# Hybrid decoder trunk: two more groups per layer by seven products, and the input's quarter sums formed in other places

## The chip, the cores and the metric

The kernel runs on one core of one Trainium2 chip. The metric is the device time of one execution in microseconds (us), the median of several runs. The parts of the core are named as in the profile: PE is TensorE's matmuls, PEld its weight loads, DVE is VectorE, ACT is ScalarE, POOL is GpSimd, and SP is SyncE, which here only issues transfers (DMAs).

## The reference

Two layers run one after the other on 512 tokens of width 2048. A layer normalises its input, multiplies it by one wide matrix `w_in` of 7696 columns, and feeds the columns to three groups of heads: a short gated convolution, a stick-breaking attention with eight heads of 128, and a gated linear attention (GLA) with four heads. Each has a gate path through SiLU. The three outputs stand side by side, go through `w_out` and are added to the layer's input.

```python
    h = _rmsnorm(x, norm_g).astype(x.dtype)
    proj = h @ w_in
    ...
    y_conv = _short_conv(cv_h, cv_b, cv_c, conv_w, conv_b) * jax.nn.silu(cv_g.astype(f32))
    ...
    y_sb = _stick_breaking(q, k, v) * jax.nn.silu(sb_g.astype(f32))
    ...
    y_gla = _rmsnorm(o, gla_on_g).reshape(b, s, GLA_W) * jax.nn.silu(gl_g.astype(f32))

    mix = jnp.concatenate([y_conv, y_sb, y_gla], axis=-1).astype(x.dtype)
    return x + mix @ w_out
```

## The kernel before, in words

**Groups of weights.** The columns of `w_in` and `w_out` are taken 256 at a time. One such block of 2048 rows by 256 columns is a group; there are 38 in a layer, 76 in all, and they are multiplied in one fixed order. In a layer it is: GLA's V0 and V1 (V1 carries the 16 low-rank columns too), GLA's Q and K, GLA's two gates G0 and G1, the first half of the convolution (its groups H, C, G, B), four times the attention's V, Q, K and gate, the second half of the convolution, and the eight groups of `w_out`.

**Precision.** Every operand is split into a high and a low float16 part, and a product is three matmuls: high by high, high by low, low by high. The splitting is work of ACT (the high part, a scaled copy) and DVE (the low part, scaled value minus high part).

**Two ways to multiply a group.** The plain way for groups whose result stands with columns on the partitions (`project_cols`, L625 to L627) takes 2 column blocks x 16 row blocks x 3 = 96 matmuls of 128x512. The other way, `seven` (L677 by columns, L680 by tokens), cuts the input into four quarters (tokens 0 to 255 and 256 to 511, rows 0 to 1023 and 1024 to 2047) and the weights into four (the two row halves, the two column blocks), and forms the four quarters of the result from seven products of sums of quarters in place of eight. By columns that is 7 x 8 x 3 = 168 matmuls of 128x256. Which groups go this way is in the table `SEVEN`; before, there are 39.

**What `seven` needs of the weights.** A plain group's two staged halves of 1 MB (tag `st`, four buffers) are split into four tiles `w` (`whi` L419, `wlo` L423, 128x1024 each). For `seven`, `right` (L428 to L452) makes seven such tiles (ACT L436, DVE L437), with four additions in place on the staged halves between them (L440, L441, L444, L445). The pool of `w` tiles has six buffers for all groups. A group is prepared about one group ahead: its squares are summed for a scale (ACT L344, an all-reduce on POOL, L357), and its tiles are made as buffers come free. The fetch of a staged half (L332, on SP) waits until the half that it overwrites has been split.

**What `seven` needs of the input.** Four sums of the input's quarters, in float16 parts and transposed. `x_sums` (L768) makes them once per layer, and it is issued behind V1's last weight split: eight additions on the normalised input `xt` in place (`column_sums`, L763 to L766, 128x1024 each), eight splits (ACT L780, DVE L781), each into a borrowed tile, and sixteen transposes by DMA on SP (L789), which write the sums into two tiles `s` that take over the buffers of `xt`. In `quarters`, sum 1 is the left operand of product 1, sum 0 of product 3, sums 2 and 3 of products 4 and 5; products 0, 2 and 6 take quarters of the input itself. The products are computed in the order 0, 1, 3, 2, 4, 5, 6.

**The results of `seven`.** Three PSUM banks `psp` serve all groups. By columns, two copies on ACT (L691, L727) and five additions on DVE (L720, L723, L731, and L735 twice), each 128x256, bring the quarters into an SBUF tile; a plain group is read from PSUM by what follows, for a gate by the chain of L820 to L827.

**Borrowed tiles.** The split sums go to tiles whose tags belong to other steps and have one or two buffers, handed on in the order of the program: `g` (the gates), `zw` and `raw` (`attd` of GLA, which POOL clears at L975; `raw` is also `Pc`, GLA's running sum of decays), `qT` and `kT` (GLA's q and k), `qp` (`att_`), `th` (GLA's `src_` and `tgt_`, which POOL clears at L907). A later tile of a tag waits until the transposes out of the borrowed one have ended.

**Order.** Up to the first layer's GLA the order of DVE and ACT is written out by hand. Behind that a planner sets the order of every queue from its own costs: by the order in the program, with weight preparation and the results of `seven` raised in priority. The queues themselves (DVE, ACT, PE, POOL, and the DMA issues of SP) run in order.

**After GLA's projections** the linear attention goes on in the background of the following groups: for each pair of heads a loop over seven levels with exponentials on ACT, products on DVE and small matmuls on PE (`mm3`, L968).

Of the kernel before, what the change touches and what calls it, by code (L numbers as in the profile page):

```python
# [11 lines left out]
ALU = mybir.AluOpType  # L12
# [20 lines left out]
CHUNKS = ((((3, 0), (2, 512)), (3, 2)), (((0, 0), (1, 128)), (0, 1)))  # L33


SEVEN = {"gla": (), "conv0": (1,), "sb": (1,2), "pairs": ((1,3),(2,3),(3,3),), "conv1": (0,1,), "out": (2, 3, 4, 5, 6), "end": (7,)}


@with_exitstack
def hybrid_trunk(ctx, tc, x, norm_g, w_in, conv_w, conv_b, sb_qn_g, sb_kn_g,  # L40
                 gla_w_up, gla_b_up, gla_on_g, w_out, out):
    nc = tc.nc
    V, S, G, T = nc.vector, nc.scalar, nc.gpsimd, nc.tensor
    depth, D = norm_g.shape
# [31 lines left out]
    def wk(shape, tag, bufs=None, dt=F32):  # L76
        return work.tile(shape, dt, tag=tag, name=nm(tag), bufs=bufs)

    def newbig(tag, shape, dt):
        return big.tile(shape, dt, tag="big", name=nm(tag))  # L80
# [13 lines left out]
    xt = [newbig("x", [P, 2, D], F32) for _ in range(2)]  # L94
# [198 lines left out]
    def plan(l, src, cols, seven):  # L293
        specs.append((l, src, cols))
        modes.append(seven)

    for l in range(depth):
        for n, cols in enumerate(([(GL_V, GW)], [(GL_V + GW, GW), (GL_LR, LR)], [(GL_Q, GW)], [(GL_K, GW)],
                                  [(GL_G, GW)], [(GL_G + GW, GW)])):
            plan(l, w_in, cols, n in SEVEN["gla"])  # L300
        for j in range(2):
            if j:
                for jj in range(4):
                    for n, c0 in ORDER[min(jj, 1)]:
                        plan(l, w_in, [(c0 + jj * GW, GW)], n in SEVEN["sb"] or (jj, n) in SEVEN["pairs"])
            for n, c0 in enumerate((CV_H, CV_C, CV_G, CV_B)):
                plan(l, w_in, [(c0 + j * GW, GW)], n in SEVEN["conv1" if j else "conv0"])
        for gi in range(NG):
            plan(l, w_out, [(gi * GW, GW)], gi in SEVEN["out"] or gi in SEVEN["end"] and l == depth - 1)
    ratio = {}  # L310
# [448 lines left out]
    def column_sums(pieces):  # L759

        tt = V.tensor_tensor
        for x11, x12, x21, x22 in pieces:
            tt(x22, x21, x22, ALU.subtract)  # L763
            tt(x21, x11, x21, ALU.subtract)
            tt(x11, x22, x11, ALU.subtract)
            tt(x12, x12, x11, ALU.add)  # L766

    def x_sums():  # L768

        for t in range(2):  # L770
            column_sums([(xt[0][:, t, :D // 2], xt[0][:, t, D // 2:], xt[1][:, t, :D // 2], xt[1][:, t, D // 2:])])
        where = ((1, 1), (0, 0), (1, 0), (0, 1))
        tags = iter((("g", 2), ("g", 2), ("zw", 1), ("raw", 2), ("qT", 2), ("qp", 1), ("th", 2), ("th", 2)))
        parts = {}
        for i in (0, 2, 1, 3):
            th, kh = where[i]
            for t in range(2):
                v = xt[th][:, t, kh * (D // 2):(kh + 1) * (D // 2)]
                parts[i, t] = a = wk([P, 2, D // 2], *next(tags), F16)
                S.activation(a[:, 0], v, AF.Copy)  # L780
                V.tensor_tensor(a[:, 1], v, a[:, 0], ALU.subtract)  # L781
        sums = {}
        for pair in ((0, 2), (1, 3)):
            b = newbig("s", [P, 2, 2, HK, 2, P], F16)
            for n, i in enumerate(pair):
                sums[i] = [b[:, n, hl] for hl in range(2)]
                for t in range(2):
                    for hl in range(2):
                        nc.sync.dma_start_transpose(sums[i][hl][:, :, t, :], parts[i, t][:, hl])  # L789
        return sums  # L790

    for l in range(depth):
# [10 lines left out]
        def toks(tag, bufs):  # L803

            if modes[cursor[0]]:
                raw = wk([P, NT, GW], tag, bufs)
                u = toks7(sums, raw)
                return [raw[:, 2 * b:2 * b + 2, :].rearrange("p t c -> p (t c)") for b in range(2)], u, raw
            return *project_toks(), None

        def gate(mx=None):

            g = wk([P, 2, seq], "g")
            ps, u = cols(g)
            nu = sm(1, "nu")
            S.activation(nu, u, AF.Copy, scale=-1.0)
            gx = sm(2, "gx")
            for c in range(2):
                a = wk([P, seq], "ga")
                S.activation(a, ps[c], AF.Exp, scale=nu)  # L820
                V.tensor_scalar(a, a, 2.0 ** 62, None, ALU.min)
                S.activation(a, a, AF.Ln, bias=1.0)
                S.activation(a, a, AF.Exp, scale=-1.0)
                if mx is None:
                    V.scalar_tensor_tensor(g[:, c, :], ps[c], u, a, ALU.mult, ALU.mult)
                else:
                    V.tensor_tensor_reduce(out=g[:, c, :], in0=ps[c], in1=a, scale=u, scalar=0.3, op0=ALU.mult,  # L827
                                           op1=ALU.max, accum_out=gx[:, c:c + 1])
            if mx is not None:
                V.tensor_tensor(mx, gx[:, 0:1], gx[:, 1:2], ALU.max)  # L830
            return g
# [37 lines left out]
        for i, bs in enumerate((slice(0, 6, 2), slice(1, 6, 2), slice(6, 8))):  # L869
            n = 3 if i < 2 else 2  # L870
# [11 lines left out]
        for p in range(2):  # L882
# [3 lines left out]
            a = wk([P, seq], "ga")  # L886
# [11 lines left out]
        if any(modes[cursor[0]:cursor[0] + 30]):  # L898
            with tc.issue_after(los[cursor[0] - 1].ins):
                sums = x_sums()  # L900
# [71 lines left out]
        for p in range(2):  # L972
# [4 lines left out]
            for li, h in enumerate(LEV[:-1]):  # L977
                b = li % 2
# [42 lines left out]
            for two, bias in ((0, (nT[:, p, 0:1], None, nT[:, p, 2:3], None)),  # L1021
                              (1, (nT01[:, p:p + 1], nT[:, p, 1:2], None, nT[:, p, 2:3]))):
                e = wk([P, 2, 256], "e")
                n = [0, 0]
# [244 lines left out]
        for j in range(4):  # L1269
# [4 lines left out]
            for gain in (None, kg[:, l, :]):  # L1274
                ps, u, raw = toks("raw", 2)
                sq = sm(8, "qs")
                made = raw is not None
                raw = raw if made else wk([P, NT, GW], "raw")
# [33 lines left out]
            g = gate(bm[:, 1:2])  # L1312
# [20 lines left out]
        if not last:  # L1333
            xt = [newbig("x", [P, 2, D], F32) for _ in range(2)]
# [129 lines left out]
```

## Time and profile before

| What | Value |
|---|---|
| median of 3 runs | 1669.94 us (1669.52 to 1670.4) |
| the profiled execution | 1670.56 us |
| its span in the trace | 1668.4 us |
| PE busy, matmuls | 1641.0 us, 98% |
| PEld busy | 1332.4 us, 80% |
| DVE busy | 1413.9 us, 85% |
| ACT busy | 1242.0 us, 74% |
| POOL busy | 72.8 us, 4% |
| HBM read, written | 179.88 MB, 14.68 MB |

The profile is one execution. Its page gives the busy time of each engine; then the costliest groups of instructions, each with line, engine, operation, what it writes and reads, shape, count, busy time in us, the mean duration of one in ns, and the engine's idle time just before them with what ended it. Other views ask the same trace by stretches of time (the windows: busy time of each engine, the granted PE clock, the DMA engines' share and rate), in order of time (the timeline), and by waits. Times in them count from the start of the span. Matmuls are pipelined: the duration of one is longer than the spacing between two, so a rate is read from start to start.

### The profile page before, as it was taken

What the parts mean: (1) busy time and instruction counts of PE and PEld (TensorE: products, weight loads), DVE (VectorE), ACT (ScalarE), POOL (GpSimd) and SP (SyncE); (2) the same over time, 40 slices, a digit from 0 to 9 for tenths busy, and PEclk for the clock granted to TensorE, in tenths of its full rate; (3) what the DMA queues carried; (4) which work ended last, traced back from release to release, by engine and by line L of the source; (5) the groups of instructions that cost most, each with busy time, mean ns of one, the idle gap of its engine ahead of it and who ended that gap; (6) DMA issues with size and microseconds to landing.
All of it is one profiled execution on the core that took longest, in us unless ns stands there. A gap on an engine that the chain in (4) does not pass through costs nothing.

```text
span 1668.4 us, 40601 instructions
## 1 busy us (share of the span) xinstructions
PE 1641.0 (98%) x17450; PEld 1332.4 (80%) x17450; DVE 1413.9 (85%) x2322; ACT 1242.0 (74%) x1711; POOL 72.8 (4%) x96
## 2 busy tenths in 40 slices
PE   8999999999999999999999999999999999999999
PEld 6744748999999986699986457589989998858999
DVE  7967888899898987888778588988999899979896
ACT  7777777697878787666867678776969696976663
POOL 0011000000000000000000100000000000000000
PEclk9999999999999999999999999999999999999999
DMA  7384331446364549244755724324464546473441
GB/s 260 101 189 115 102 98 60 130 98 163 111 152 120 152 126 268 81 159 153 229 145 135 175 70 127 102 82 110 118 156 118 156 117 158 126 235 102 153 153 52
DMA packets 308099, 227.58 MB, mean 136 GB/s; under 512 B 127650, under 2 KB 301004, under 8 KB 307408
## 3 DMA queue, kind: packets, MB, share of 16 engines
q1 hardware_dynamic: 298912, 215.55, 46.6%
q10 hardware_dynamic: 9008, 9.45, 1.8%
q8 instruction: 136, 2.23, 0.6%
q14 instruction: 43, 0.35, 0.1%
HBM read 179.88 MB, written 14.68 MB: 117 GB/s over the span
## 4 chain that ended last, share of the span: by engine, by line
PE 25%; DVE 11%; issue 10%; ACT 6%; DMA 2%; POOL 1%; SPq 1%; ACTq 0%; POOLq 0%; DVEq 0%
PE psp L680 5%; PE psp L677 5%; PE psp L653 3%; DVE w L437 3%; ACT w L436 2%; PE psp L627 2%; PE psp L625 2%; PE psp L626 2%; PE psp L642 1%; PE psp L643 1%; PE psp L641 1%; ACT junk L344 1%; DMA st<-in_w_in_dram 1%; DVE th L963 1%; DVE w L423 1%
## 5 line engine op out<-in xcount | busy, mean ns | idle before, releaser
L436 ACT ACTIVATE w<-st,ws 128x1024 f16<-128x1024 f32 x273 | 305.2, 1141 | 145.5 <-DVE st L441 59.9
L437 DVE SCALAR_TENSOR_TENSOR w<-st,ws,w 128x1024 f16<-128x1024 f32 x273 | 344.7, 1280 | 63.8 <-ACT w L436 60.8
L344 ACT ACTIVATE junk<-st 128x2048 uint8<-128x2048 f32 x150 | 284.9, 1899 | 14.8 <-DMA st<-in_w_out_dram 6.8
L677 PEld LDWEIGHTS <-w 128*128 128x128 f16 x2352 | 230.2, 98 | 32.1 <-DVE u L720 2.1
L642 PE MATMUL psp<-w,act 128*128 128x256 f16 x896 | 244.0, 273 | 0.0
L641 PE MATMUL psp<-w,act 128*128 128x256 f16 x896 | 243.8, 273 | 0.0
L643 PE MATMUL psp<-w,act 128*128 128x256 f16 x896 | 243.7, 273 | 0.0
L680 PE MATMUL psp<-w,act 128*128 128x128 f16 x3600 | 215.0, 219 | 4.4 <-DVE w L437 2.1
L625 PE MATMUL psp<-act,w 128*128 128x512 f16 x576 | 218.3, 379 | 0.9 <-DVE gx L827 0.9
L627 PE MATMUL psp<-act,w 128*128 128x512 f16 x576 | 218.3, 379 | 0.0
L626 PE MATMUL psp<-act,w 128*128 128x512 f16 x576 | 218.3, 379 | 0.0
L680 PEld LDWEIGHTS <-act 128*128 128x128 f16 x3600 | 205.3, 98 | 8.0 <-issue 4.6
L423 DVE SCALAR_TENSOR_TENSOR w<-st,ws,w 128x1024 f16<-128x1024 f32 x148 | 187.5, 1279 | 26.5 <-ACT w L419 26.1
L419 ACT ACTIVATE w<-st,ws 128x1024 f16<-128x1024 f32 x144 | 161.9, 1140 | 23.4 <-PE psp L627 15.3
L680 PE MATMUL psp<-w,s 128*128 128x128 f16 x2688 | 156.3, 219 | 0.4 <-DVE vv L723 0.3
L677 PE MATMUL psp<-s,w 128*128 128x256 f16 x1344 | 156.1, 274 | 0.0
L680 PEld LDWEIGHTS <-s 128*128 128x128 f16 x2688 | 152.0, 98 | 1.8 <-issue 1.6
L357 POOL PARTITION_ALL_REDUCE wgm<-wm x75 | 57.5, 767 | 1439.4 <-ACT junk L344 1270.4
L677 PE MATMUL psp<-act,w 128*128 128x256 f16 x1008 | 118.9, 273 | 0.0
L653 PE MATMUL psp<-w,act 128*128 128x256 f16 (+1 forms) x960 | 112.3, 278 | 4.2 <-ACT act L515 1.6
L653 PEld LDWEIGHTS <-act 128*128 128x128 f16 x960 | 94.4, 99 | 20.6 <-issue 2.5
L626 PEld LDWEIGHTS <-w 128*128 128x128 f16 x576 | 56.3, 98 | 66.7 <-issue 1.2
(358 smaller groups left out, 2651.0 us busy)
## 6 DMA issues: line engine op xcount, KB each, us to landing
st<-in_w_in_dram SPq DMA_DIRECT2D x120, 1024.0 KB, 5.8
st<-in_w_out_dram SPq DMA_DIRECT2D x32, 1024.0 KB, 5.5
m<-mixd SPq DMA_DIRECT2D x24, 256.0 KB, 5.5
x<-in_x_dram SPq DMA_DIRECT2D x4, 1024.0 KB, 12.1
qT<-in_x_dram ACTq DMA_DIRECT2D x8, 512.0 KB
qT<-xs ACTq DMA_DIRECT2D x8, 512.0 KB, 3.8
out_dram<-kT SPq DMA_DIRECT2D x16, 256.0 KB, 2.2
mixd<-e SPq DMA_DIRECT2D x12, 256.0 KB
```

The lines of the kernel that those rows point to most:

```text
L344: squares[i] = S.activation(junk(HK * GW).rearrange("p (k n) -> p k n", k=HK), staged[i][h], AF.Square, accum_out=peak[i][:, h:h + 1])
L436: his.setdefault(i, []).append(S.activation(hi, x, AF.Copy, scale=scales[i]))
L437: V.scalar_tensor_tensor(lo, x, scales[i], hi, ALU.mult, ALU.subtract)
L625: T.matmul(o, wh, xh[:, k, :, :], start=st_, stop=False)
L626: T.matmul(o, wh, xl[:, k, :, :], start=False, stop=False)
L627: T.matmul(o, wl, xh[:, k, :, :], start=False, stop=en)
L641: T.matmul(o, xh[:, k, t, :], wh, start=k == 0 and t % 2 == 0, stop=False, skip_group_check=True)
L642: T.matmul(o, xh[:, k, t, :], wl, start=False, stop=False, skip_group_check=True)
L643: T.matmul(o, xl[:, k, t, :], wh, start=False, stop=k == lastk, skip_group_check=True)
L653: T.matmul(o[:, :n], a_[:, k, t, :], wview(w, part, k, n), start=i == 0 and k == 0, stop=i == 2 and k == KT - 1)
L677: T.matmul(o[:, :2 * P], ww, x[xi][:, k, :, :], start=first, stop=final, skip_group_check=True)
L680: T.matmul(o[:, t * P:(t + 1) * P], x[xi][:, k, t, :], ww, start=first, stop=final, skip_group_check=True)
```

## The change

Three edits. `SEVEN["gla"]` goes from none to groups 4 and 5, so that GLA's gates G0 and G1 are multiplied by `seven` in both layers: 43 groups in place of 39. The four additions of `x_sums` give the same four sums in other places: sums 0 and 1 now stand in the second half of the tokens (`xt[1]`), sums 2 and 3 in the first (`xt[0]`), and one of the four is a `scalar_tensor_tensor`. The splits and the transposes are issued in the order 1, 0, 2, 3 in place of 0, 2, 1, 3, out of other borrowed tiles: two of `th`, two of `g`, `zw`, `kT`, `qT`, `qp`. `raw` is no longer borrowed, `kT` is.

```diff
-SEVEN = {"gla": (), "conv0": (1,), "sb": (1,2), "pairs": ((1,3),(2,3),(3,3),), "conv1": (0,1,), "out": (2, 3, 4, 5, 6), "end": (7,)}
+SEVEN = {"gla": (4,5,), "conv0": (1,), "sb": (1,2), "pairs": ((1,3),(2,3),(3,3),), "conv1": (0,1,), "out": (2, 3, 4, 5, 6), "end": (7,)}
...
     def x_sums():
 
         for t in range(2):
-            column_sums([(xt[0][:, t, :D // 2], xt[0][:, t, D // 2:], xt[1][:, t, :D // 2], xt[1][:, t, D // 2:])])
-        where = ((1, 1), (0, 0), (1, 0), (0, 1))
-        tags = iter((("g", 2), ("g", 2), ("zw", 1), ("raw", 2), ("qT", 2), ("qp", 1), ("th", 2), ("th", 2)))
+            a, b = (xt[0][:, t, n * (D // 2):(n + 1) * (D // 2)] for n in range(2))
+            c, d = (xt[1][:, t, n * (D // 2):(n + 1) * (D // 2)] for n in range(2))
+            V.tensor_tensor(a, a, c, ALU.subtract)
+            V.tensor_tensor(c, c, d, ALU.subtract)
+            V.scalar_tensor_tensor(d, d, -1.0, a, ALU.mult, ALU.subtract)
+            V.tensor_tensor(b, b, d, ALU.add)
+        where = ((1, 0), (1, 1), (0, 0), (0, 1))
+        tags = iter((("th", 2), ("th", 2), ("g", 2), ("g", 2), ("zw", 1), ("kT", 2), ("qT", 2), ("qp", 1)))
         parts = {}
-        for i in (0, 2, 1, 3):
+        for i in (1, 0, 2, 3):
             th, kh = where[i]
             for t in range(2):
                 v = xt[th][:, t, kh * (D // 2):(kh + 1) * (D // 2)]
...
         sums = {}
-        for pair in ((0, 2), (1, 3)):
+        for pair in ((1, 0), (2, 3)):
             b = newbig("s", [P, 2, 2, HK, 2, P], F16)
```

## The prediction

> **What bounds the kernel now.** I read the page's head first, then the waits of PE.
>
> ```profile
> span 1668.4 us, 40601 instructions
> PE 1641.0 (98%) x17450; PEld 1332.4 (80%) x17450; DVE 1413.9 (85%) x2322; ACT 1242.0 (74%) x1711; POOL 72.8 (4%) x96
> ```
>
> ```profile
> PE psp L680 <- DVE w L437: 3.6, 4, 1.1
> ...
> PE psz L968 <- DVE th L963: 1.5, 4, 0.4
> ...
> PE psp L625 <- DVE gx L827: 0.9, 1, 0.9
> ```
>
> PE is idle for 1668.4 - 1641.0 = 27.4 us in all. Its largest wait on DVE is 3.6 us in four pieces, behind weight splits; GLA's small matmuls wait 1.5 us for it. So the number of matmul columns that PE streams sets the time, as long as DVE, the next engine, keeps up. Whether it does is a question of the stage, not of its 85%. The change acts in GLA's projections, so I read windows there, and in the stretch behind:
>
> ```profile
> 92.98:157.97 64.99, 64.10 (x315) 29.71 (x314) 39.69 (x88) 45.12 (x63) 8.42 (x9) 1.00 0.67 157
> 920.00:982.50 62.50, 62.50 (x292) 28.32 (x290) 38.71 (x86) 43.86 (x60) 6.59 (x8) 1.00 0.60 153
> 157.97:280.57 122.60, 121.63 (x895) 79.90 (x893) 111.43 (x221) 94.19 (x165) 2.56 (x5) 1.00 0.25 78
> ```
>
> After the length of the stretch stand the busy times of PE, PEld, DVE, ACT and POOL, the granted clock, and the DMA share and rate. The first row holds the groups K, G0 and G1 of layer 0, the second those of layer 1, the third the convolution's first half and the attention's first V behind them. PE is full in all three, at the full clock. DVE is 61% busy in the first two (25.3 and 23.8 us idle) and 91% in the third (11.2 us idle).
>
> **PE's gain.** Two pieces of the timeline give the rates, from start to start.
>
> ```profile
> 114.14 0.38 PE L625 MATMUL psp<-act,w 128*128 128x512 f16 x1
> ...
> 134.86 0.38 PE L625 MATMUL psp<-act,w 128*128 128x512 f16 x1
> ```
>
> ```profile
> 600.31 2.78 PE L677 MATMUL psp<-act,w 128*128 128x256 f16 x24
> 602.93 5.40 PE L677 MATMUL psp<-s,w 128*128 128x256 f16 x48
> ```
>
> The first pair is G0 itself: 96 matmuls in 20.72 us, 215.8 ns each. In the second, 24 matmuls of half the width take 2.62 us, 109.2 ns each. A gate by `seven` is 168 x 109.2 ns = 18.34 us, which is 2.38 us less; four gates give -9.5 us. That is less than an eighth of 82.9 us (10.4), since a half-width matmul costs slightly more than half. Also, the wait of 0.9 us at L625 above goes: there G1 wanted a PSUM bank that G0's gate chain was still reading, and `seven` empties its banks with short copies and additions. Together -10.4 us.
>
> The weight loads grow from 96 to 168 in a gate. One takes 98 ns, and yet matmuls of 109.2 ns follow each other with no room left, so it lies beside them and I cost it at nothing:
>
> ```profile
> L677 PEld LDWEIGHTS <-w 128*128 128x128 f16 x2352 | 230.2, 98 | 32.1 <-DVE u L720 2.1
> ```
>
> The Trainium skill speaks against this (TensorE: Matmul & The Clock Gate, section The mechanism): a weight load overlaps matmuls in flight only when it goes to other row groups, and these fill all rows. By that rule the 72 extra loads of a gate would stand on the path, and the sum would be a loss; this trace, with 98 ns inside a spacing of 109.2 ns, does not follow it.
>
> **What DVE and ACT get.**
>
> ```profile
> L436 ACT ACTIVATE w<-st,ws 128x1024 f16<-128x1024 f32 x273 | 305.2, 1141 | 145.5 <-DVE st L441 59.9
> L437 DVE SCALAR_TENSOR_TENSOR w<-st,ws,w 128x1024 f16<-128x1024 f32 x273 | 344.7, 1280 | 63.8 <-ACT w L436 60.8
> ```
>
> ```profile
> L440 DVE TENSOR_TENSOR st<-st,st 128x1024 f32<-128x1024 f32 x39 | 47.7, 1222 | 18.2 <-DMA st<-in_w_in_dram 7.4 <-ACT junk L344 5.8 <-ACT w L436 3.2
> ...
> L720 DVE TENSOR_TENSOR u<-psp,s 128x256 f32<-128x256 f32 x28 | 11.6, 413 | 0.1
> ...
> L691 ACT ACTIVATE s<-psp 128x256 f32<-128x256 f32 x28 | 10.4, 371 | 3.0 <-PE psp L677 1.6 <-PE psp L680 1.4
> ```
>
> Per gate, DVE gets three more weight splits (3 x 1.28), four additions of 1.22 and five small ones of 0.41 (L723, L731 and L735 taken at L720's duration): 3.84 + 4.88 + 2.07 = 10.8 us. ACT gets 3 x 1.14 + 2 x 0.37 = 4.2 us. Per layer that is 21.6 us on DVE, against idle time of 25.3 or 23.8 us in a stretch that becomes 4.8 us shorter. DVE will be nearly full there, and since part of its idle time is waiting in a chain, some work of GLA will slide into the next stretch, which has 11.2 us free. Prepared weights are not late: G0's seventh tile needs a buffer that its own product 0 frees 2.6 us after the start, and is used as the last of seven, some 13 us later.
>
> What this costs PE the trace of before cannot show, so I bound it. The nearest row below is the stretch behind (0.97 us of PE idle in 122.6, 0.8%). The nearest above is the output stage, with five groups by `seven` in a row:
>
> ```profile
> 720.00:834.00 114.00, 110.16 (x1821) 107.73 (x1820) 92.77 (x128) 82.20 (x125) 4.29 (x7) 1.00 0.56 178
> ```
>
> There PE idles 3.84 us in 114, 3.4%. On about 60 us per layer that is 0.5 to 2.0 us. A bound below nothing has a reason too: if GLA's chain runs earlier (next part), the idle 0.97 us of the stretch behind can go. I take 1.0 us per layer, between the rows and nearer to the lower, because only two such groups stand in a row here: +2.0 us.
>
> **The sums of the input.** Now they are needed in G0. By the rates above, G0 of layer 0 (start 114.14) needs sum 1 at 116.8, sum 0 at 119.4, sum 2 at 124.6, sum 3 at 127.2.
>
> ```profile
> 83.99 5.18 SPq L789 DMA_TRANSPOSE s<-g  x3
> ...
> 108.83 1.23 SPq L789 DMA_TRANSPOSE s<-raw  x1
> 110.83 0.37 SPq L332 DMA_DIRECT2D st<-in_w_in_dram  x1
> 113.31 1.23 SPq L789 DMA_TRANSPOSE s<-raw  x1
> ...
> 124.73 5.39 SPq L789 DMA_TRANSPOSE s<-th  x2
> ```
>
> ```profile
> 107.76 1.05 ACT L780 ACTIVATE raw<-x 128x1024 f16<-128x1024 f32 x1
> ```
>
> ```profile
> DMA to landing us min/median/max: 3.2/3.4/6.6
> ```
>
> Six transposes went out from 83.99; the other ten came from 113.31 on, because one split waited for a `raw` buffer until 107.76. Without `raw` all splits end near 85 (one DVE split of about 1.2 us moves forward). The ten took 130.12 - 113.31 = 16.8 us, 1.7 each with a load among them, so sixteen end near 113, and land by 120 at the latest: 7 us before sum 3 is wanted. Layer 1 is tighter:
>
> ```profile
> 901.18 2.61 SPq L789 DMA_TRANSPOSE s<-g  x2
> ...
> 910.35 6.51 SPq L789 DMA_TRANSPOSE s<-zw  x2
> ```
>
> Its first six took 15.7 us with two loads, 2.6 each. Sixteen at that rate from 902 end at 944 and land by 951; at 1.7 they land by 936. G0 starts there at 920.0 + 20.7 = 940.7 and wants sum 1 at 943.3, sum 3 at 953.8. So both layers arrive in time, and I cost this at nothing; with the slowest rate 3 us of cover are left. The one `scalar_tensor_tensor` costs 0.06 us more than an addition.
>
> The moved transposes also pass POOL's queue:
>
> ```profile
> 99.85 0.95 POOL L975 MEMSET zw<- 128x1024 f32 x1 [12.25 <-DMA s<-zw]
> ...
> 101.08 0.48 POOL L357 PARTITION_ALL_REDUCE wgm<-wm  x1
> ...
> 126.13 1.80 POOL L907 MEMSET th<- 128x2048 f16 x1 [6.04 <-DMA s<-th]
> ...
> 132.22 1.80 POOL L907 MEMSET th<- 128x2048 f16 x1 [3.90 <-DMA s<-th]
> ```
>
> `zw`'s transposes become ninth and tenth instead of fifth and sixth, so its clearing moves from 99.85 to 106 to 109, and behind it in order stands the all-reduce of 101.08 for G1's scale. G1's tiles find no free buffer before 117, so this is covered by 8 us. `th`'s transposes become the first four: its clearings no longer wait until 126 and 132, and GLA's level loop starts some 6 us earlier. That is DVE work moved to where DVE has room; it is no gain by itself.
>
> **The sum.** -9.5 - 0.9 + 2.0 = -8.4 us. On the profiled execution: 1670.56 (2.16 us around its span) - 8.4 = 1662.2. The median of the runs is 0.6 below that execution, so I predict 1661.5. About 0.2% (3.3 us) can be told from no change.
>
> **The rivals.**
>
> *DVE becomes the bound* (0.13). Work that slides out of the gates' stretch finds the next one 91% full; DVE then trails PE, and PE waits on evictions and on GLA's small matmuls through both. For: 21.6 us into 24. Against: the stretch behind runs at 91% with PE idle only 0.97 us, and GLA starts earlier. Priced at the output stage's 3.4% over 60 + 118 us: 6.0 us per layer, less the 1.0 there now, twice: +10.0. With -10.4 that is -0.4: 1669.5, the same time.
>
> *SP's queue in the wrong order* (0.08, slower). The fetch for the group behind G1 now waits until G0's seventh tile has been split, not before 116.8 + 1.14 + 1.28 = 119.2. If the planner puts it on SP ahead of the transposes of sums 2 and 3, they wait behind it, though their data has long been ready: eight at 1.7 us end at 132.8 and land at 136.2, so product 5 starts 9 us late. In both layers +18: 1661.5 + 18 = 1679.5. It decides as soon as a fetch that waits for the seventh tile stands before the last eight transposes. For: such a fetch (110.83) stood among the transposes before. Against: those transposes were waiting themselves; now they are ready 30 us earlier.
>
> *Weight loads on the path* (0.01). If the 72 extra loads of 98 ns in each gate stood in line, four gates would get 28.2 us: 1661.5 + 28.2 = 1689.7. Groups by `seven` run today without this.
>
> That the change does not do what it says I rule out: the gates call the same branch on the table as the convolution's groups, and the four sums are term by term the old ones.
>
> **Numbers.** My forecast, 1658 to 1666, has 0.75. The lower end takes the new waits at nothing and lets the 0.97 us in both layers go: 1669.9 - 10.4 - 1.9 = 1657.6, say 1658. Beside the rivals' 0.22, 0.03 is left over: 0.02 to a larger gain, 0.01 to a loss. The range reaches halfway into the first rival, to 1668.5. Faster by over 0.2%: 0.77. Same: 0.13. Slower: 0.10.
>
> **What would show it.** Right: L677 with 672 more matmuls and L625 to L627 with 384 fewer; G0 to G1 near 18.4 us from start to start; PE busy about 1632; no wait of PE on a transpose into `s`; the clearings of `th` before 115; DVE near 1457 us, over 90% busy from 93 to 153. Wrong: PE waits of more than 3 us per layer on DVE between G0 and the attention's first group (first rival), or on a DMA into `s` inside G0, with a fetch on SP just before the late transposes (second).

## The result, and the profile after

| | median | lowest to highest, runs | beside it, before | ratio, 95% |
|---|---|---|---|---|
| changed kernel | 1674.32 us | 1673.65 to 1677.36, 7 | 1669.52 us | 1.0030 (1.0021 to 1.0039) |

The change makes the kernel slower by 0.3%, 4.8 us by the medians; forecast were 8.4 us the other way. The profiled execution took 1673.65 us, 2.25 of them around its span. The head of the page:

```profile
span 1671.4 us, 41284 instructions
...
PE 1634.1 (98%) x17738; PEld 1361.0 (81%) x17738; DVE 1450.8 (87%) x2370; ACT 1254.9 (75%) x1731; POOL 76.6 (5%) x96
```

PE has 6.9 us less to do than before, and yet the span is 3.0 us longer: PE is idle for 37.3 us where it was 27.4. PE's waits (line waited for: us in total, times, longest) say on whom:

```profile
PE psz L973 <- DVE th L968: 4.6, 6, 1.9
...
PE psp L677 <- DVE vv L723: 3.5, 2, 1.9
...
PE psp L677 <- DVE u L720: 1.5, 2, 1.1
```

L973 (L968 before), GLA's small matmuls, waited 1.5 us and now waits 4.6. The waits for `vv` and `u` at L677 are new: 5.0 us, in G0 of both layers, for the additions that empty a PSUM bank. The wait of 0.9 us at L625 is gone. G0 of layer 0 on PE's timeline (start, length; in brackets the idle time and what ended it):

```profile
114.34 2.78 PE L677 MATMUL psp<-act,w 128*128 128x256 f16 x24
...
125.40 1.80 PE L677 MATMUL psp<-s,w 128*128 128x256 f16 x15 [0.42 <-DVE u L720]
129.12 3.76 PE L677 MATMUL psp<-s,w 128*128 128x256 f16 x33 [1.92 <-DVE vv L723]
...
135.34 0.28 PE L973 MATMUL psz<-th,th 128*128 128x128 f16 x2
```

G0 takes 21.00 us, and two gaps make nearly all that is over the 18.34 forecast. No wait is for a sum `s`: the sums are in time. Is DVE full, then? The windows (length, then PE, PEld, DVE, ACT, POOL busy) of the whole stretch, of G0 alone, and of the stretch behind:

```profile
93.10:152.49 59.39, 57.05 (x439) 41.63 (x437) 48.37 (x92) 45.11 (x64) 5.31 (x6) 1.00 0.56 138
114.34:135.34 21.00, 18.66 (x170) 16.43 (x169) 19.50 (x44) 16.65 (x25) 1.36 (x1) 1.00 0.33 101
152.49:276.10 123.61, 121.35 (x896) 80.23 (x893) 108.57 (x215) 95.59 (x161) 2.86 (x6) 1.00 0.29 91
```

In G0 it is, 93%. Over the stretch it is 81% busy, not the forecast 90%: 11.0 us idle, 6.9 of them in the 21.24 us ahead of G0, where it is busy for 14.34. So DVE stands still first and is short of time afterwards. Where it stands, in layer 0 and then in layer 1 (DVE's timeline; the row at 912.25 is G0's, the other two of L440 are G1's):

```profile
101.96 1.23 DVE L440 TENSOR_TENSOR st<-st,st 128x1024 f32<-128x1024 f32 x1 [3.71 <-DMA st<-in_w_in_dram]
...
104.57 0.21 DVE L360 TENSOR_SCALAR wq<-wgm 128x1 f32<-128x1 int32 x1 [1.26 <-POOL wgm L357]
```

```profile
912.25 1.23 DVE L440 TENSOR_TENSOR st<-st,st 128x1024 f32<-128x1024 f32 x1 [3.76 <-DMA st<-in_w_in_dram]
...
928.40 1.23 DVE L440 TENSOR_TENSOR st<-st,st 128x1024 f32<-128x1024 f32 x1 [2.36 <-DMA st<-in_w_in_dram]
```

L440 is the first of a gate's four additions; it needs both staged halves of the weights. The one that it waits for at 101.96 is issued on SP at 95.09:

```profile
85.11 8.47 SPq L794 DMA_TRANSPOSE s<-g  x3
93.69 1.31 SPq L794 DMA_TRANSPOSE s<-zw  x1
95.09 1.35 SPq L332 DMA_DIRECT2D st<-in_w_in_dram  x1
96.50 2.35 SPq L794 DMA_TRANSPOSE s<-zw  x1
98.90 4.17 SPq L794 DMA_TRANSPOSE s<-kT  x2
```

It stands right behind four transposes that take 9.8 us to issue; before, the second half of G1's weights went out at 89.27:

```profile
89.27 0.53 SPq L332 DMA_DIRECT2D st<-in_w_in_dram  x1
```

On POOL, the all-reduce for G1's scale stands behind the clearing of `zw`:

```profile
103.06 0.95 POOL L980 MEMSET zw<- 128x1024 f32 x1 [6.66 <-DMA s<-zw]
104.13 0.41 POOL L357 PARTITION_ALL_REDUCE wgm<-wm  x1
```

In this kernel the clearing hardly delays the all-reduce, since what it reduces is ready only at 103.97 us, behind the same late load (the squares on ACT, L344).

### The profile page after: what moved, and what is told of

It is laid out like the page before. It is cut to its first block, busy times and chain, and to the rows that moved or that the text cites. A ratio compares the mean times of both kernels' runs of the same rounds, so it can differ in the third digit from the quotient of the medians.

```text
span 1671.4 us, 41284 instructions
## 1 busy us (share of the span) xinstructions
PE 1634.1 (98%) x17738; PEld 1361.0 (81%) x17738; DVE 1450.8 (87%) x2370; ACT 1254.9 (75%) x1731; POOL 76.6 (5%) x96
## 4 chain that ended last, share of the span: by engine, by line
issue 19%; PE 15%; DVE 12%; ACT 5%; DMA 3%; SPq 1%; POOL 1%; ACTq 0%; POOLq 0%; DVEq 0%
PE psp L680 4%; DVE w L437 3%; PE psp L677 2%; PE psp L627 2%; PE psp L625 2%; PE psp L626 2%; DMA st<-in_w_in_dram 1%; ACT junk L344 1%; ACT w L436 1%; SPq L794 1%; POOL wgm L357 1%; PE psp L653 1%; DMA st<-in_w_out_dram 1%; DVE w L423 1%; DVE st L445 1%
## 5 line engine op out<-in xcount | busy, mean ns | idle before, releaser
L436 ACT ACTIVATE w<-st,ws 128x1024 f16<-128x1024 f32 x301 | 336.3, 1141 | 155.3 <-DVE st L441 71.0
L437 DVE SCALAR_TENSOR_TENSOR w<-st,ws,w 128x1024 f16<-128x1024 f32 x301 | 380.3, 1279 | 56.8 <-ACT w L436 54.1
L677 PEld LDWEIGHTS <-w 128*128 128x128 f16 x3024 | 295.8, 98 | 45.3 <-issue 7.5
L344 ACT ACTIVATE junk<-st 128x2048 uint8<-128x2048 f32 x150 | 284.9, 1900 | 27.4 <-DMA st<-in_w_in_dram 24.1
L680 PEld LDWEIGHTS <-act 128*128 128x128 f16 x3600 | 205.5, 98 | 9.0 <-issue 4.5
L677 PE MATMUL psp<-s,w 128*128 128x256 f16 x1728 | 200.4, 274 | 5.0 <-DVE vv L723 3.5
L423 DVE SCALAR_TENSOR_TENSOR w<-st,ws,w 128x1024 f16<-128x1024 f32 x132 | 168.0, 1279 | 25.1 <-ACT w L419 24.6
L626 PE MATMUL psp<-act,w 128*128 128x512 f16 x448 | 169.8, 379 | 0.0
L627 PE MATMUL psp<-act,w 128*128 128x512 f16 x448 | 169.8, 379 | 0.0
L625 PE MATMUL psp<-act,w 128*128 128x512 f16 x448 | 169.6, 379 | 0.0
L419 ACT ACTIVATE w<-st,ws 128x1024 f16<-128x1024 f32 x128 | 144.7, 1140 | 22.9 <-PE psp L627 14.9
L677 PE MATMUL psp<-act,w 128*128 128x256 f16 x1296 | 151.7, 273 | 0.3 <-DVE g L731 0.3
L653 PEld LDWEIGHTS <-act 128*128 128x128 f16 x960 | 94.5, 99 | 20.9 <-issue 2.5
L642 PEld LDWEIGHTS <-act 128*128 128x128 f16 x896 | 87.7, 98 | 10.9 <-issue 0.6
```

Of the source, the lines that this page charges most:

```text
L344: squares[i] = S.activation(junk(HK * GW).rearrange("p (k n) -> p k n", k=HK), staged[i][h], AF.Square, accum_out=peak[i][:, h:h + 1])
L436: his.setdefault(i, []).append(S.activation(hi, x, AF.Copy, scale=scales[i]))
L437: V.scalar_tensor_tensor(lo, x, scales[i], hi, ALU.mult, ALU.subtract)
L625: T.matmul(o, wh, xh[:, k, :, :], start=st_, stop=False)
L626: T.matmul(o, wh, xl[:, k, :, :], start=False, stop=False)
L627: T.matmul(o, wl, xh[:, k, :, :], start=False, stop=en)
```

## Theories

*Load* is the first rival of the prediction: 10.8 us of DVE work per gate are too much, wherever they stand. *Queue* (called *gate* in later expectations): work that waits at the head of an in-order queue (G1's weights behind the transposes on SP, the all-reduce behind the clearing on POOL) makes DVE stand idle before G0, so that the same work is late in G0.

All runs in one table; "before" is the kernel before on the same chip.

| run | median us | before | ratio, 95% |
|---|---|---|---|
| e1_sums_alone | 1669.45 | 1668.76 | 1.0003 (0.9994 to 1.0011) |
| e2_gates_old_sums | 1671.88 | 1668.76 | 1.0017 (1.0009 to 1.0026) |
| e3_no_additions | 1666.22 | 1668.76 | 0.9984 (0.9974 to 0.9994) |
| e4_weights_first | 1670.22 | 1668.76 | 1.0008 (0.9999 to 1.0017) |
| e5_clear_late | 1666.00 | 1668.87 | 0.9982 (0.9973 to 0.9991) |
| e6_additions_on_pool | 1712.57 | 1668.87 | 1.0262 (1.0248 to 1.0276) |
| e7_second_gate_only | 1667.99 | 1668.87 | 0.9993 (0.9984 to 1.0002) |
| e8_load_alone | 1670.27 | 1668.87 | 1.0009 (1.0000 to 1.0018) |
| e9_clear_alone | 1673.00 | 1668.98 | 1.0024 (1.0015 to 1.0033) |
| e10_queues_no_additions | 1660.68 | 1668.98 | 0.9949 (0.9937 to 0.9961) |
| e11_plain_gates_queues | 1668.02 | 1668.98 | 0.9995 (0.9987 to 1.0004) |
| e12_small_splits_first | 1665.95 | 1668.98 | 0.9980 (0.9971 to 0.9988) |
| e13_same_load_off_chain | 1670.59 | 1669.41 | 1.0005 (0.9996 to 1.0014) |
| e14_off_chain_old_queues | 1678.92 | 1669.41 | 1.0057 (1.0044 to 1.0069) |

Differences between two runs are taken from their ratios, times 1669.5 us; each carries about 2 us of uncertainty.

## Experiments: the parts of the change

**The sums alone.**

```diff
-SEVEN = {"gla": (4,5,), ...
+SEVEN = {"gla": (), ...
```

> The new x_sums alone: the kernel after with SEVEN gla empty, so both gates of the linear attention stay plain (six product groups of 512 columns) and DVE does none of the gates' additions, while the input's quarter sums are formed and transposed as in the changed kernel. Two theories of the 4.8 us that the change cost instead of the forecast gain. Load: the gates' additions and extra evictions (10.8 us of DVE for each gate) pile up on DVE at G0, and its evictions and the small matmuls of the linear attention come late. Queue: the sixteen transposes, now bunched between 76 and 109 us, stand on SP's queue ahead of the gates' staged weights, which land late; DVE and ACT wait for them in order, and have too much left when G0's results come. Load expects this run level with the kernel before, 1669.5 us, 1668.5 to 1670.5, since the load is gone. Queue expects a part of the loss here, since ACT's squares and the splits of plain weights stand behind the same transfers: 1670.5 to 1672.5, with the second half of G1's weights issued near 95 us as in the changed kernel.

Level with before (1.0003). Moving the sums costs nothing while the gates are plain. This is what load expected; queue's 1 to 3 us lie at the edge of the interval. The waits are there all the same: G1's second half goes out at 95.69 us, and DVE stands 7.89 us for G1's scale. In the kernel before, DVE already stood 5.08 us for another all-reduce behind the clearing of `zw`. So DVE's standing still costs PE nothing that can be told while the gates are plain.

**The gates with the old sums.**

```diff
-SEVEN = {"gla": (), ...
+SEVEN = {"gla": (4,5,), ...
```

This edit is to the kernel before.

> The gates by seven products with the sums formed as in the kernel before (SEVEN gla = (4,5) in it, x_sums unchanged). In the kernel before the last eight transposes were issued between 108.8 and 126.9 us, and G0 begins near 114 and needs the first pair of sums at 117. Both theories expect PE to wait in G0 for a sum, 8 to 13 us per layer: 1669.5 - 9.5 + 16 to 26 gives 1676 to 1686. If it is faster than the changed kernel's 1674.3, the bunching of the transposes costs more than late sums, which speaks for queue; load expects it slower than the changed kernel by the whole wait.

Both theories missed: 1671.88 is 4 us below the least that they allowed. PE waits for a sum twice, both times in layer 0:

```profile
PE psp L677 <- DMA s<-qp: 4.4, 1, 4.4
...
PE psp L677 <- DMA s<-th: 0.9, 1, 0.9
```

Sums that come late cost 5.3 us of waits here. Behind the longer one the granted clock is 0.65 for 3 us, and 48 matmuls take 7.08 us where 5.40 is the rate. And yet, by the ratios, the kernel is if anything faster than with the moved sums (1.0017 against 1.0030, intervals that overlap). So the sums, moved as they are here, don't help the gates, which speaks for queue.

**The changed kernel without the gates' additions.**

```diff
-        V.tensor_tensor(b, b, d, ALU.add)
-        V.tensor_tensor(a, a, b, ALU.add)
+        if not gate_:
+            V.tensor_tensor(b, b, d, ALU.add)
+            V.tensor_tensor(a, a, b, ALU.add)
```

The other two, L444 and L445, are left out in the same way.

> The changed kernel without the four additions that form each gate's weight sums (left out: the sums of the gates' weight pieces, so these products use unsummed pieces). DVE loses 4 x 1.22 = 4.9 us per gate, 19.6 us in all; PE, the transfers and the order of the transposes stay. Load expects the PE waits of G0 and behind it to fall to those of the kernel before: 1674.3 less 8 to 12, so 1662 to 1666.5. Queue expects DVE to wait for the same staged halves at its next instruction, the splits: at most 3 us off, 1671 to 1674.5.

By the ratios 7.7 us off the changed kernel, as load expected. The time alone doesn't tell apart why: the additions are DVE's load and also the instruction that stands at the head of DVE's queue in the waits. The trace does in part. In layer 0 DVE now stands 6.86 us for G1's scale, so the wait moved to the next instruction, as queue said, and still the time fell. What fell is therefore not this wait. The planner's order of PE, DVE and ACT changed with the edit, too, and may have a part in it.

## Experiments: the order of the queues

**Weights ahead of twelve transposes on SP.**

```diff
+            if tag == "kT" and sums:
+                with tc.issue_after(fetched[cursor[0] + 1].ins):
+                    turn((0, 2, 3))
```

`turn` issues the transposes of the sums named; `fetched` holds the last fetch of each group.

> The changed kernel with twelve of the sixteen transposes queued on SP behind the second half of G1's staged weights (four stay ahead); the order of the instructions on PE, DVE and ACT is the same as in the changed kernel, instruction for instruction. G1's second half, issued at 95.1 us in the changed kernel, should be issued near 88.5, when K's splits have freed its buffer, and land near 95 instead of 101.9; the transposes then run from 89 to about 108, and both pairs of sums are still there when G0 wants them (117 and 125). Queue expects DVE's 3.7 us wait at G1's first addition to go, in layer 1 also those of 3.8 and 2.4 us, G0 to take 18.5 to 19.5 us instead of 21.0, and the time 1666 to 1670. Load expects the same additions to crowd DVE at G0 and the time within 1.5 us of the changed kernel: 1673 to 1675.5.

By the ratios 3.7 us off the changed kernel with no instruction of PE, DVE or ACT added, removed or reordered. Queue gave 1666 to 1670 and load 1673 to 1675.5; 1670.22 is 0.2 us over queue's range and well below load's. Three fetches now go out together, the last of them by 88.4, and G1's addition no longer waits for a transfer, in either layer. G0's in layer 1, which queue wanted gone too, still waits 3.12 us where it was 3.76. But the wait did not end, it moved on (SP's, DVE's and POOL's timelines; line numbers are 2 to 10 higher here):

```profile
81.17 7.18 SPq L334 DMA_DIRECT2D st<-in_w_in_dram  x3
88.40 9.11 SPq L799 DMA_TRANSPOSE s<-g  x4
```

```profile
97.56 1.22 DVE L442 TENSOR_TENSOR st<-st,st 128x1024 f32<-128x1024 f32 x1 [0.16 <-ACT junk L346]
...
103.75 0.21 DVE L362 TENSOR_SCALAR wq<-wgm 128x1 f32<-128x1 int32 x1 [4.84 <-POOL wgm L359]
```

```profile
102.39 0.95 POOL L990 MEMSET zw<- 128x1024 f32 x1 [6.85 <-DMA s<-zw]
103.31 0.41 POOL L359 PARTITION_ALL_REDUCE wgm<-wm  x1
```

DVE now stands 4.84 us for G1's scale, which the all-reduce delivers, which is queued on POOL behind the clearing of `zw`, which waits for the transposes that read `zw`.

**The clearing behind the all-reduce as well.**

```diff
-            G.memset(attd, 0.0)
+            with tc.issue_after(reduced[cursor[0] - 1].ins):
+                G.memset(attd, 0.0)
```

> The kernel of e4_weights_first with one edit more: GpSimd's clearing of zw stands behind the all-reduce of G1's weight maximum instead of ahead of it; PE, DVE, ACT and SP keep their orders instruction for instruction. In e4 the wait for the staged weights went, but DVE then stood 4.84 us (layer 0) and 5.66 us (layer 1) at the scale of G1's weights, behind the all-reduce, which stood in GpSimd's queue behind the clearing of zw, which waits for the transposes that read zw. Gate (what stands at the head of an in-order queue decides): these 10.5 us of DVE come free ahead of G0, most of the waits in G0 go and those of the linear attention's small matmuls shrink, 2 to 4 us off e4: 1666 to 1668.5. Load (the sum of DVE's work decides): the waits move to the next instruction, within 1 us of e4's 1670.2: 1669 to 1671.

1666.0, as queue expected: 8.0 us off the changed kernel by the ratios, and faster than the kernel before (0.9982, interval wholly below 1). From e4 to e5 nothing differs in the orders of PE, DVE, ACT and SP; on POOL the clearing and the all-reduce changed places, once per layer. In layer 0 G0 now runs without a gap, 132.14 - 113.80 = 18.34 us, the forecast to the hundredth:

```profile
100.34 0.41 POOL L359 PARTITION_ALL_REDUCE wgm<-wm  x1 [4.53 <-ACT junk L346]
102.31 0.95 POOL L991 MEMSET zw<- 128x1024 f32 x1 [1.56 <-DMA s<-zw]
```

```profile
113.80 2.78 PE L679 MATMUL psp<-act,w 128*128 128x256 f16 x24
116.42 5.40 PE L679 MATMUL psp<-s,w 128*128 128x256 f16 x48
121.66 2.78 PE L679 MATMUL psp<-act,w 128*128 128x256 f16 x24
124.28 5.40 PE L679 MATMUL psp<-s,w 128*128 128x256 f16 x48
129.52 2.78 PE L679 MATMUL psp<-act,w 128*128 128x256 f16 x24
132.14 0.28 PE L983 MATMUL psz<-th,th 128*128 128x128 f16 x2
```

GLA's small matmuls still wait:

```profile
PE psz L983 <- DVE th L978: 4.4, 6, 1.9
```

**The clearing alone**, on the changed kernel.

> The changed kernel with only the second edit of e5_clear_late: GpSimd's clearing of zw behind the all-reduce of G1's weight maximum, the transposes on SP left as in the changed kernel. There the clearing ended at 104.0 us and the second half of G1's weights landed at 101.9 us, so the all-reduce could run only 1 to 2 us earlier. Gate, with two waits in a row of which the later one counts: within 1.5 us of the changed kernel (1672.5 to 1674.5), although the same edit gave 4 us on top of e4. If it gives 3 us or more here as well, the two edits act on separate waits and the account of e5 is wrong.

As expected, 1673.0, 1.0 us by the ratios. Alone the two edits give 3.7 and 1.0, together 8.0: the two waits stand one behind the other, and the later one decides.

**Both edits with plain gates.** The edit is that of e1, on the kernel of e5.

> The kernel of e1_sums_alone (both gates plain) with both edits of e5_clear_late on SP's and GpSimd's queues: what the edits alone are worth without the gates by seven. Gate: little waits there, so level with e1 and the kernel before, 1667.5 to 1669.5, and e5 is faster than this run by a part of the 9.5 us that the gates' rate is worth on PE less the waits that e5 still has at the linear attention's small matmuls (about 5 us more than in the kernel before): 2.5 to 5 us. If this run is as fast as e5, the gain of e5 comes from the edits and not from the gates.

0.9995, level with before. So the edits are worth nothing that can be told by themselves (1.3 us over e1). e5 is 2.2 us faster than this run by the ratios, a little under the 2.5 to 5 expected, and that is what the gates by `seven` bring, of 9.5 on PE: PE is busy for 9.7 us less than here (1630.0 and 1639.7) and idle for 6.3 us more (34.1 and 27.8).

## Experiments: the load

**Only the second gate**, on the kernel of e5 (`"gla": (5,)`).

> The kernel of e5_clear_late with only the second gate (G1) by seven products; G0 stays plain. PE's busy time gains 2 x 2.38 = 4.75 us instead of 9.5, DVE carries 10.8 us per layer less. Load: hardly any PE wait on DVE over those of the kernel before is left, so 1668.8 - 4.75 = 1664 to 1666, faster than e5. Gate: e5 has lost its waits already and gains twice as much on PE, so this run is 2 to 4 us slower than e5.

1.8 us slower than e5 by the ratios: nearer to what queue expected, though the difference is no larger than its uncertainty. One gate brings 0.3 us over e11, which is nothing that can be told, and two bring 2.2, at the edge of it.

**The load beside plain gates**, on the kernel of e1.

```diff
+        if specs[i][1] is w_in and specs[i][2][0][0] in (GL_G, GL_G + GW):
+            for n in range(9):
+                e, f = (staged[i][h][:, :, (n % 2) * P:(n % 2 + 1) * P] for h in range(2))
+                V.tensor_tensor(e, e, f, ALU.add)
```

> The kernel of e1_sums_alone (both gates plain) with nine in-place additions of 1.22 us on each gate's staged weights put on DVE behind that gate's splits: 11 us of DVE per gate, where the products by seven added 10.8, and no other change of PE's work or of the transfers (the additions come after the last reader of the staged values, so the products are the same). Load: slower than e1's 1669.5 by what the changed kernel lost to PE waits, 6 to 12 us: 1675 to 1681. Queue: DVE's idle time around the gates takes the additions in, less than 3 us: 1669.5 to 1672.5.

1.0 us over e1 by the ratios, where load expected 6 to 12. The windows of the gates' stretch, first of e1, then of this run:

```profile
93.00:158.00 65.00, 64.19 (x301) 29.11 (x300) 38.65 (x86) 45.50 (x63) 5.78 (x7) 1.00 0.64 156
```

```profile
93.00:158.00 65.00, 63.26 (x312) 29.29 (x310) 56.92 (x105) 43.50 (x62) 5.89 (x7) 1.00 0.60 148
```

DVE takes 18.3 us more, 88% in place of 59%, and PE loses 0.9. The waits of e1 stand in this kernel too (3.64 us for G1's scale). So beside plain products neither the sum of DVE's work in the stretch nor these waits set the time.

**G1's additions on GpSimd**, on the kernel of e5.

```diff
+        E_ = G if specs[i][1] is w_in and specs[i][2][0][0] == GL_G + GW else V
...
-        V.tensor_tensor(b, b, d, ALU.add)
+        E_.tensor_tensor(b, b, d, ALU.add)
```

> The kernel of e5_clear_late with G1's four additions of staged weights on GpSimd instead of DVE (G0's stay on DVE). DVE loses 4.9 us per layer just ahead of G0. Load: without the additions of both gates the changed kernel lost 8 us, so a half of them gives 2 to 4 us off e5, if GpSimd has G1's sums ready before G1 begins (135 us); GpSimd's price for an addition of 128x1024 is not known here, and its queue holds the all-reduces that DVE waits for, so if one addition takes over 4 us the scales come late and the run is slower than e5 by 2 us and more. Gate: within 1 us of e5, or slower for the queue.

Far slower, 47 us over e5 by the ratios, and not by the price of an addition, which is 2.33 us:

```profile
102.57 2.33 POOL L443 TENSOR_TENSOR st<-st,st 128x1024 f32<-128x1024 f32 x1 [6.83 <-ACT w L439]
110.93 0.41 POOL L359 PARTITION_ALL_REDUCE wgm<-wm  x1 [6.03 <-issue]
```

```profile
111.37 0.21 DVE L362 TENSOR_SCALAR wq<-wgm 128x1 f32<-128x1 int32 x1 [13.52 <-POOL wgm L359]
```

Between an addition and an all-reduce GpSimd stood 6.03 us waiting for nothing that the profile shows, and DVE 13.52 us for the scale. It says nothing on load; what DVE shows is a wait at the head of its queue once more. The 47 us are not accounted for one by one: PE's busy time is 12.6 us up as well, at a mean granted clock of 0.987.

**Ordered queues without the additions**, the edits of e3 and e5 together.

> The kernel of e5_clear_late without the four additions of each gate (the sums of the gates' weight pieces left out, so these products use unsummed pieces). Gate: the additions cost the changed kernel 8 us because they stood at the head of DVE's queue in the waits; with the waits gone they are covered, and this run gains 0 to 3 us on e5's 1666.0: 1663 to 1666. Load: 19.6 us of DVE less give about as much as in e3, 6 to 9 us: 1657 to 1660.

1660.68, 5.5 us below e5 by the ratios: under load's 6 to 9 and over queue's 0 to 3. Both missed. PE is as busy as in e5 (1629.8 and 1630.0) and idles 5.1 us less. GLA's small matmuls now wait 2.5 us for `th` in place of 4.4, and waits of 3.2 us for `g`, `e` and `zw` are gone:

```profile
PE psz L986 <- DVE th L981: 2.5, 2, 1.2
```

**Those matmuls' operands first**, on the kernel of e5.

```diff
-            S.activation(hi, e, AF.Copy)
-            V.tensor_tensor(lo, e, hi, ALU.subtract)
+            with tc.high_priority():
+                S.activation(hi, e, AF.Copy)
+                V.tensor_tensor(lo, e, hi, ALU.subtract)
```

The same is done in `split_tgt`.

> The kernel of e5_clear_late with the linear attention's splits into halves (the copies on ACT and subtractions on DVE that feed its small matmuls) put at high priority, so that they stand ahead of weight splits and additions of later groups on DVE and ACT. In e5 PE still waits for them at 180 us (1.1), 188 (0.6) and 277 (1.9) in layer 0 and for 1.5 us in layer 1. If these waits come from weight work standing ahead in DVE's order, 3 to 5 us go: 1661 to 1663.5. If the splits are late because their own inputs are (the exponentials, the products before), within 1 us of e5, or slower where the weights behind them come late.

Level with e5: the waits at 180, 188 and 277 us stand as they were (1.13, 0.59 and 1.91). The splits are not late for their own place in the order.

**The same load behind the gate's last split**, on e10 and on e3.

```diff
         part(c)
+        if gate_:
+            for o, x, y in ((b, b, d), (a, a, b), (c, c, a), (a, a, d)):
+                V.tensor_tensor(o, x, y, ALU.add)
```

> The kernel of e10_queues_no_additions (queues in order, the gates' weight sums left out, so these products use unsummed pieces) with four in-place additions of the same size put on DVE for each gate behind its last split, where nothing reads their result but the next load of the staged tile. DVE's work is that of e5_clear_late; only the place differs: behind the gate's chain from staged weights to splits to products instead of inside it. Load (the sum of DVE's work costs the 5.3 us between e10 and e5): level with e5, 1665 to 1667. Place (the additions cost because the splits and products stand behind them): level with e10, 1660 to 1662.5.

> The kernel of e3_no_additions (transposes and clearing queued as in the changed kernel, the gates' weight sums left out, so these products use unsummed pieces) with the same four additions per gate behind its last split. DVE's work is that of the changed kernel. Load: level with the changed kernel, 1672 to 1675. Place: level with e3, 1665 to 1668.

Place is refuted: with nothing of their own gate behind them, the additions cost more than inside its chain, 9.3 us over e10 and 12.2 over e3 by the ratios, 3.8 and 4.5 more than load expected. New waits appear in e13 (PE's waits), for ACT's copies as well:

```profile
PE psz L989 <- DVE th L984: 4.0, 5, 1.1
PE psz L989 <- ACT th L983: 3.8, 5, 2.0
...
PE psp L685 <- DVE w L439: 1.3, 1, 1.3
```

With gates by `seven`, then, these additions cost PE time wherever they were tried. In this place they also hold the staged halves longer: the fetch behind the transposes goes out at 127.64 us, in e10 at 117.63. That may be the rest, but it was not separated. The planner moved other instructions of DVE, ACT and PE too in e3, e8, e10, e13 and e14, so a part of their differences from the kernels they were made from may be its order.

The queues' part is free of this. In three pairs of kernels whose PE, DVE and ACT run the same instructions in the same order, the two edits of e5 give 8.0 us (changed kernel to e5), 5.8 (e3 to e10) and 8.7 (e14 to e13); with plain gates (e1 to e11) they give 1.3. And why the load costs 1 us beside plain gates and 5.5 or more beside gates by `seven` stays open: `seven` asks DVE to empty a bank every few us, which plain gates don't, and that is a likely reason, not a shown one.

## Why the prediction was wrong

The rate on PE was right. G0 takes 18.34 us wherever nothing holds it (e5), the 0.9 us at L625 are gone, and the extra weight loads lie beside the matmuls (PEld 28.6 us up, G0 at its forecast). L677 has its 672 matmuls more, and PE's busy time, 1634.1 with the clock's fall told below, is near the 1632 forecast. DVE's, 1450.8, is 6 us under the 1457 forecast. The sums of the input come in time, `th` is cleared at 80.90 and 83.56, before 115 as said; no fetch holds the transposes, so the second rival did not happen.

Three steps failed, all on what the change costs the other engines.

*"So both layers arrive in time, and I cost this at nothing; ..."* The sums do. But the step priced the moved transposes by their own arrival and not by what they pass on SP: G1's second staged half goes out 5.8 us later. It looked for a fetch that holds transposes (the second rival) and not for the reverse. (A slip in its working changes nothing: the transposes from 113.31 to 130.12 are nine and not ten, so 1.9 us each and not 1.7.)

*"G1's tiles find no free buffer before 117, so this is covered by 8 us."* The clearing moved to 103.06, even earlier than the 106 to 109 forecast. But the cover was that of G1's tiles; DVE's queue runs in order, and G1's addition (101.96) and scale (104.57) stand in it ahead of G0's third split and last two additions (106.26 to 110.06), which wait with them. The late load comes first and the clearing second: mended alone, the clearing gives 1.0 us (e9), within the uncertainty; with the load mended as well the time falls by 8.0 (e5).

*"I take 1.0 us per layer, between the rows and nearer to the lower ... +2.0 us."* With the queues in order, the additions cost 5.5 us (e10 to e5, the planner's order with them), and what else DVE and ACT get is put at e10's distance from the forecast gain: -8.5 by its ratio against -10.4, a remainder of 1.9. That makes 7.4 in place of 2.0. Both bounds came from stretches of the kernel before; what the moved transposes would do to a queue lay outside them.

The sum by the runs: -10.4 + 1.9 + 5.5 + 8.0 = +5.0 us, which must give the measured ratio (1.0030), since the steps are differences of ratios. Taken in the other order, the additions come to 7.7 (changed kernel to e3) and the queues to 5.8 (e3 to e10): their total of 13.5 holds, its division does not. The first rival was right that PE comes to wait on DVE, and in part wrong on why: over the stretch DVE was not full (81% where it wanted 90%) but idle first, while the cost of the additions speaks for it. It gave 1669.5; the changed kernel is 4.8 us beyond it.

## What to carry to other kernels

When a step is moved, ask of each in-order queue it passes not only whether the moved work arrives, but who now stands behind it, and whether that is at the head of another in-order queue: here a 1 MB load behind transposes, an all-reduce behind a clearing, and DVE behind both. An engine that is 61% busy may have its idle time in waits, and new work that stands behind such a wait comes late: beside plain gates the waits (e1) and the added work (e8) cost next to nothing, beside gates by `seven` both cost. When one wait is removed, look at once for the wait behind it: here one edit gave 3.7 us, the other 1.0, both 8.0.

## What the runs showed of the hardware

**A clock that falls behind two gaps.** In G0 of layer 1 of the changed kernel (PE's timeline, then windows with the granted clock after POOL's count):

```profile
952.46 0.81 PE L677 MATMUL psp<-s,w 128*128 128x256 f16 x6 [1.07 <-DVE u L720]
954.88 6.41 PE L677 MATMUL psp<-s,w 128*128 128x256 f16 x42 [1.60 <-DVE vv L723]
```

```profile
953.00:955.00 2.00, 0.40 (x5) 0.20 (x3) 2.00 (x5) 0.11 (x1) 0.00 (x0) 1.00 0.98 336
955.00:958.00 3.00, 3.00 (x16) 2.18 (x15) 3.00 (x6) 1.95 (x2) 0.00 (x0) 0.52 0.35 115
958.00:961.00 3.00, 3.00 (x27) 2.58 (x25) 1.51 (x3) 3.00 (x6) 0.00 (x0) 0.91 0.01 3
```

42 matmuls at 109.2 ns would take 4.75 us with the last one's tail; they took 6.41. So 2.67 us of idle time within 3.5 us cost 1.66 us more by the clock, which was granted at 0.52. In e9 the same place, with gaps of 1.01 and 1.60 us, shows 0.78 and 0.66 in the windows from 952 and from 955; in G0 of layer 0 of e3, gaps of 0.78 and 1.43 us show 0.63 from 128 to 131 us. In e4, with 0.16 and 1.60, and in layer 0 of the changed kernel, with 0.42 and 1.92 and 1.80 us of matmuls between them, the clock stays at 1.00. The Trainium skill (TensorE: Matmul & The Clock Gate, Part 1: The HAM clock gate) tells of half rate behind an idle window of about 3.4 us that runs free of the kernel; here two gaps shorter than that, with 0.81 us of matmuls between them, were enough.

**A transpose that issues slowly beside a load.** The eight transposes out of `g` in the changed kernel (duration min, median, max in ns):

```profile
L794 SPq DMA_TRANSPOSE s<-g x8: 1308/2679/4703, 82.2 to 915.1; - x8
```

Among loads of 1 MB the issue of one took up to 4.70 us. In layer 0 the load issued at 95.09 ends DVE's wait at 101.96; the two transposes from 98.90 take 4.17 us beside it, and the four from 103.11, behind it, 5.41, so 1.35 each. All that stands behind a transpose on SP waits with it.

**GpSimd between an addition and an all-reduce** stood 6.03 us in layer 0 of e6 and 5.88 us in layer 1, with no wait that the profile shows, though its spans on POOL are rough. Between a clearing and an all-reduce there was no gap (e4: 102.39 and 0.95 us, then 103.31).
